# GpSimd sums of squares, and a halved last unit ahead of a norm, in a two-layer float32 encoder

## The chip, the cores and the metric

The kernel runs on 1 core of one Trainium2 chip. The time is the device time of one execution in microseconds (us), here the median of several runs. Engines are named as in the profile: PE is TensorE's matmul, PEld its weight load, DVE is VectorE, ACT is ScalarE, POOL is GpSimd, SP is SyncE, which issues the transfers.

## The reference

An encoder of two layers works on 256 tokens of width 2048. The part that matters here:

```python
for l in range(DEPTH):
    mod = (c_act @ w_mod[l] + b_mod[l]).reshape(bn, 6, d)
    ...
    h = layer_norm(x) * (1.0 + scale_m) + shift_m
    proj = h @ w_in[l]
    uv, q_c, kv_c, k_r, sb, sc, sh, ag = jnp.split(proj, IN_SPLITS, axis=-1)
    y_a = gmlp_mixer(uv, ...)
    y_b = mla_mixer(q_c, kv_c, k_r, ...)   # begins with rms_norm(q_c), rms_norm(kv_c)
    y_c = short_conv_mixer(sb, sc, sh, ...)
    y_d = conformer_conv(ag, ...)
    y = jnp.concatenate([y_a, y_b, y_c, y_d], axis=-1) @ w_out[l]
    x = layer_norm(ALPHA * x + (1.0 + gate_m) * y, post_mix_g[l], post_mix_b[l])

    h = layer_norm(x) * (1.0 + scale_f) + shift_f
    y = conv_ffn(h, ...)                   # ends in @ w_down
    x = layer_norm(ALPHA * x + (1.0 + gate_f) * y, post_ffn_g[l], post_ffn_b[l])
```

`rms_norm(x)` divides each token's row by the root of its mean square (384 columns for `q_c`, 256 for `kv_c`). Each layer has two products that end in a residual step and a LayerNorm over the 2048 columns of a token: `@ w_out` and `@ w_down`.

## The kernel before, in words

**Tokens and layout.** The 256 tokens are two tiles of 128 rows, `X[0]` and `X[1]`, kept on chip (in the instruction lists below they are called `x_97` and `x_98` at the place shown). The mixing groups A to D work with channels on the partitions and 256 tokens in the free direction.

**Products.** Most float32 products are made of three: ScalarE casts a block of weights to a rounded `hi` (L458), VectorE subtracts to get the rest, `lo` (L459), and TensorE adds hi*hi, hi*lo and lo*hi. Weight tiles are called `whi`/`wlo`, or `thi`/`tlo` where they lie in another pool. Some blocks are plain float32 instead (`wexact`), which the profile counts as two records for each product. All products go through one line, L83.

**Order.** The code is written as a stream: `stream` issues the load of one unit of weights and then runs the work that was pending, so loads run one unit ahead. Code order is not engine order: the framework's scheduler orders each engine's instructions by its own estimate of when they are ready, then every engine runs its list in order, waiting on semaphores.

**`out_proj`** makes both `@ w_out` (named o in the profile) and `@ w_down` (named d), so it runs four times; I name these o0, d0, o1, d1. The 2048 output columns go in three chunks, `CHUNKS = ((0, 1024), (1024, 512), (1536, 512))`. A bank of PSUM holds 512 columns of one token tile; `o_153600` is the bank of columns 1536 to 2047 of tile 0, `o_153610` that of tile 1. In the last chunk the last four units are kept in `state["tail"]`, and `done` runs them for tile 0 and then for tile 1, so that tile 0 ends early. A unit of this chunk has 4 blocks of 128 rows: 12 products of 512 columns for a tile (4 where the weights are plain float32).

After that, `finish` and `finish_bank` evacuate each tile's bank: `yg` = PSUM * gate (L704), `x` = ALPHA * x + `yg` (L707), and the statistics of the 512 columns (bn_stats, L710). Then the norm of the tile: `second(0)` for tile 0, `norm(1)` for tile 1. These aggregate the statistics, scale the rows and hand them to the next stage, which scales again (`xn`, L86) and transposes on TensorE (L597). At the end of the program (`then` is None) both tiles go through `norm`, which sends each 512 columns to the output; there tile 1 is the last work. An order dependency keeps tile 1's evacuation behind tile 0's norm, except at the end of the program.

**`mix_b`** starts with five squares of 128x256 (`sqB`, L1050, three for `q_c` and two for `kv_c`, two squares to a tile of 512 columns). Their sums over channels are one-column products against ones into `ps_ss`: for each token tile three accumulate for `q_c` and two for `kv_c`, ten in all. VectorE makes `rr` out of them (L1069, L1072), and GpSimd takes the power -0.5 (L114). TensorE fills waits here with products of group C (`C_c`).

Of the kernel before, what the change touches and what calls it, by code (L numbers as in the profile page):

```python
# [10 lines left out]
ALU = mybir.AluOpType  # L11
AX = mybir.AxisListType

P = 128
# [40 lines left out]
def encoder_kernel(ctx: ExitStack, tc: tile.TileContext, A: dict, consts: bass.AP, out: bass.AP):  # L55
# [20 lines left out]
    def ms_tile(name):  # L76
        return msp.tile([P, 512], F32, tag="ms", name=name)
# [39 lines left out]
    X = []  # L117
# [548 lines left out]
    def out_proj(l, w, src, order, gate_of, name, post_g, post_b, before, then, plain={}, bg=0):  # L666

        nkt = len(order)
        stats = [new_stats(f"{name}{t}") for t in range(2)]
        box, kept = {}, {}  # L670

        def products(t, item, ps, u, nk):
            parts, acts = item
# [19 lines left out]
        evacs = []  # L693

        def finish(t, ps, c0):
            for i in range(len(ps[t])):
                finish_bank(t, i, ps, c0)

# [91 lines left out]
        for c0, width in CHUNKS:  # L790
            last = c0 + width == D
            nk = 2048 // width
            units = nkt // nk
            state = {"tail": []}

            def load(u, c0=c0, width=width, nk=nk, units=units, last=last):
                kt = order[nk * u]
                assert order[nk * u : nk * u + nk] == list(range(kt, kt + nk))
                spare = nk if last and units - 4 <= u < units - 2 else 0
                exact = u < plain.get(c0, 0)  # L800
                parts = weights(w, kt, nk, c0, width, exact, spare)
                s4 = src[kt // 4]
                if exact:
                    return parts, [(s4[:, kt % 4 + k, :], None) for k in range(nk)]
                acts = []
                for k in range(0, nk, 2):
                    pair = kept.get(kt + k)
                    if pair is None:
                        pair = act_pair("a")
                        split(pair, s4[:, kt % 4 + k : kt % 4 + k + 2, :])  # L810
                        if nkt == KT:
                            kept[kt + k] = pair
                    for j in range(2):
                        acts.append([h[:, j, :] for h in pair[:2]])
                return parts, acts

            def unit(item, u, state=state, c0=c0, width=width, nk=nk, last=last, units=units):
                if u == 0:
                    state["ps"] = [
                        [acc_tile(f"{name}_{c0}{t}{i}") for i in range(width // 512)] for t in range(2)  # L820
                    ]
                if last and u >= units - 4:
                    state["tail"].append((item, u))
                    if evacs:
                        evacs.pop(0)()
                    return
                for t in range(2):
                    products(t, item, state["ps"], u, nk)
                if evacs:
                    evacs.pop(0)()  # L830

            for u in range(units):
                stream(lambda: load(u), lambda item, u=u, unit=unit: unit(item, u), bg, not last)

            def done(state=state, c0=c0, nk=nk, last=last):
                if c0 == 0:
                    box["gate"] = gate_of()
                if c0 + 512 == D - 512:
                    gains()
                for t in range(2):  # L840
                    for item, u in state["tail"]:
                        products(t, item, state["ps"], u, nk)
                while evacs:
                    evacs.pop(0)()
                if not last:
                    evacs.extend(
                        lambda t=t, i=i: finish_bank(t, i, state["ps"], c0)
                        for t in range(2)
                        for i in range(len(state["ps"][t]))
                    )  # L850
                    evacs.pop(0)()
                    return
                if before is not None:
                    before()
                for t in range(2):
                    finish(t, state["ps"], c0)
                    (norm if t == 1 or then is None else second)(t)
                if then is not None:
                    then(box)

            pending.append(done)


    def mixers(l, w_in, Y, hF=None, between=None):
# [163 lines left out]
        def mix_b(cps, _):  # L1028
# [30 lines left out]
            kc, ks = tmp_tile("kc"), None  # L1059
            dve.tensor_tensor(out=kc[0:64, 0:S], in0=ps[0:64, o : o + S], in1=cosT[0:64, :], op=ALU.mult)  # L1060
            dve.tensor_tensor(out=kc[0:64, S : 2 * S], in0=ps[0:64, o : o + S], in1=sinT[0:64, :], op=ALU.mult)
            ps = ms_tile("ps_ss")
            for t in range(2):
                for j in range(3):
                    mm(ps[:, t : t + 1], sqs[j][:, t * P : (t + 1) * P], ones[:, 0:1], j == 0, j == 2)
                for j in range(2):
                    mm(ps[:, 2 + t : 3 + t], sqs[3 + j][:, t * P : (t + 1) * P], ones[:, 0:1], j == 0, j == 1)
            rr = smallp.tile([P, 8], F32, tag="rr", name="rr")
            dve.tensor_scalar(  # L1069
                out=rr[:, 0:2], in0=ps[:, 0:2], scalar1=1.0 / Q_LORA, scalar2=RMS_EPS, op0=ALU.mult, op1=ALU.add  # L1070
# [551 lines left out]
```

## Time and profile before

| | |
|---|---|
| time, median of 3 runs | 2278.2 us (2276.4 to 2282.6) |
| profiled execution: its own time | 2274.61 us |
| its span in the trace | 2272.8 us |
| mean granted clock of TensorE | 0.994 |
| data moved | 605.19 MB, mean 266 GB/s |

All durations of the trace are from the one profiled execution, which lies 3.6 us under the median of the runs. Start times count from the start of the span. Layer 0 runs to about 1187 us (d0's norm), layer 1 behind it.

### The profile page before, as it was taken

What the parts mean: (1) busy time and instruction counts of PE and PEld (TensorE: products, weight loads), DVE (VectorE), ACT (ScalarE), POOL (GpSimd) and SP (SyncE); (2) the same over time, 40 slices, a digit from 0 to 9 for tenths busy, and PEclk for the clock granted to TensorE, in tenths of its full rate; (3) what the DMA queues carried; (4) which work ended last, traced back from release to release, by engine and by line L of the source; (5) the groups of instructions that cost most, each with busy time, mean ns of one, the idle gap of its engine ahead of it and who ended that gap; (6) DMA issues with size and microseconds to landing.
All of it is one profiled execution on the core that took longest, in us unless ns stands there. A gap on an engine that the chain in (4) does not pass through costs nothing.

```text
span 2272.8 us, 31376 instructions
## 1 busy us (share of the span) xinstructions
PE 2229.4 (98%) x12311; PEld 1919.6 (84%) x12311; DVE 1780.5 (78%) x2195; ACT 1107.0 (49%) x1652; POOL 35.1 (2%) x65
## 2 busy tenths in 40 slices
PE   7999999999999999999999999999999999999998
PEld 5788886788888888888789999889888888888886
DVE  5778988878888888989977899887775565565776
ACT  3356642354455444544554434545544454454553
POOL 0011000000000000000000000000000000000000
PEclk9999999999999999999999999999999999999999
DMA  9999699778888888899867677775675555555554
GB/s 350 388 371 361 254 327 360 245 275 315 310 313 313 309 317 325 300 343 328 296 235 251 203 242 248 281 269 178 232 258 185 190 187 198 185 187 197 187 188 148
DMA packets 228717, 605.19 MB, mean 266 GB/s; under 512 B 14661, under 2 KB 27189, under 8 KB 210901
## 3 DMA queue, kind: packets, MB, share of 16 engines
q1 hardware_dynamic: 227784, 602.30, 74.2%
q8 instruction: 96, 1.57, 0.3%
q0 software_dynamic: 784, 0.90, 0.1%
q14 instruction: 53, 0.43, 0.0%
HBM read 601.05 MB, written 2.10 MB: 265 GB/s over the span
## 4 chain that ended last, share of the span: by engine, by line
PE 89%; DVE 6%; DMA 2%; issue 1%; ACT 1%; POOL 0%; SPq 0%; DVEq 0%; ACTq 0%; POOLq 0%
PE g_c L83 22%; PE v_c L83 22%; PE d L83 19%; PE o L83 7%; PE C_c L83 4%; PE D_c L83 4%; PE B_c L83 2%; DVE wlo L459 1%; PE U_c L83 1%; PE E L83 1%; PE E_c L83 1%; PE U L83 1%; PE V L83 1%; DMA wmod<-in_w_mod_dram 1%; DVE macc L251 1%
## 5 line engine op out<-in xcount | busy, mean ns | idle before, releaser
L458 ACT CAST whi<-wraw 128x1024 fp32r<-128x1024 f32 (+1 forms) x632 | 643.3, 1043 | 751.6 <-PE g_c L83 221.7
L459 DVE TENSOR_TENSOR wlo<-wraw,whi 128x1024 fp32r<-128x1024 f32 (+1 forms) x632 | 750.3, 1213 | 302.7 <-ACT whi L458 283.1
L83 PE MATMUL d<-whi,a 128*128 128x512 f32 x1344 | 388.5, 390 | 2.3 <-ACT whi L458 2.3
L251 DVE SCALAR_TENSOR_TENSOR macc<-wmod,cact,macc 128x2048 f32<-128x2048 f32 (+2 forms) x174 | 353.7, 2033 | 24.4 <-DMA wmod<-in_w_mod_dram 23.7
L83 PE MATMUL v_c<-hT,whi 128*128 128x512 f32 (+1 forms) x1456 | 343.1, 383 | 0.0
L83 PE MATMUL g_c<-hT,whi 128*128 128x512 f32 (+1 forms) x1344 | 313.3, 380 | 0.0
L83 PEld LDWEIGHTS v_c<-hT,whi 128*128 128x128 f32 x1456 | 264.5, 189 | 48.5
L83 PEld LDWEIGHTS d<-whi,a 128*128 128x128 f32 x1344 | 251.7, 188 | 55.7 <-ACT whi L458 3.5
L83 PEld LDWEIGHTS g_c<-hT,whi 128*128 128x128 f32 x1344 | 243.4, 189 | 43.2
L83 PE MATMUL d<-wlo,a 128*128 128x512 f32 x672 | 233.5, 390 | 1.7 <-DVE wlo L459 1.7
L83 PE MATMUL v_c<-hT,wlo 128*128 128x256 f32 x1400 | 190.7, 283 | 0.0
L83 PEld LDWEIGHTS v_c<-hT,wlo 128*128 128x128 f32 x1400 | 183.1, 191 | 6.6
L83 PE MATMUL g_c<-hT,wlo 128*128 128x256 f32 x1280 | 175.8, 283 | 0.0
L83 PEld LDWEIGHTS g_c<-hT,wlo 128*128 128x128 f32 x1280 | 168.2, 191 | 5.9
L83 PEld LDWEIGHTS d<-wlo,a 128*128 128x128 f32 x672 | 126.1, 188 | 30.5 <-DVE wlo L459 4.3
L478 ACT CAST a<-g 128x512 fp32r<-128x512 f32 x132 | 80.7, 619 | 81.9 <-PE d L83 80.2
L83 PE MATMUL o<-whi,a 128*128 128x512 f32 x384 | 110.5, 392 | 0.5 <-ACT whi L458 0.5
L479 DVE TENSOR_TENSOR a<-g,a 128x512 fp32r<-128x512 f32 x132 | 87.5, 683 | 5.4 <-ACT a L478 5.4
L251 DVE SCALAR_TENSOR_TENSOR qacc<-wmod,cact,qacc 128x1024 f32<-128x1024 f32 (+1 forms) x75 | 80.3, 1071 | 11.6 <-DMA wmod<-in_w_mod_dram 9.2
L83 PEld LDWEIGHTS o<-whi,a 128*128 128x128 f32 x384 | 72.0, 188 | 16.9 <-ACT whi L458 1.3
L83 PE MATMUL D_c<-hT,whi 128*128 128x256 f32 x432 | 83.0, 292 | 2.2 <-ACT hT L478 1.6
L1381 DVE SCALAR_TENSOR_TENSOR u<-g,pf,u 128x254 f32<-128x254 f32 (+1 forms) x176 | 73.5, 478 | 0.0
(370 smaller groups left out, 2618.1 us busy)
## 6 DMA issues: line engine op xcount, KB each, us to landing
wraw<-in_ffn_w_up_dram SPq DMA_DIRECT2D x168, 1024.0 KB, 4.9
wmod<-in_w_mod_dram SPq DMA_DIRECT2D x134, 1024.0 KB, 6.0
wraw<-in_ffn_w_down_dram SPq DMA_DIRECT2D x88, 1024.0 KB, 5.3
wraw<-in_w_in_dram SPq DMA_DIRECT2D x33, 1024.0 KB, 7.5
wmod<-in_w_mod_dram SPq DMA_DIRECT2D x64, 512.0 KB, 9.2
wraw<-in_w_out_dram SPq DMA_DIRECT2D x26, 1024.0 KB, 5.2
wmod<-in_w_mod_dram SPq DMA_DIRECT2D x32, 768.0 KB, 8.0
wexact<-in_w_in_dram SPq DMA_DIRECT2D x46, 512.0 KB, 7.4
```

The costliest lines, as they stand in the source:

```text
L83: pe.matmul(o, lhsT, rhs, start=start, stop=stop, skip_group_check=True)
L251: i = dve.scalar_tensor_tensor(out=acc, in0=w, scalar=col, in1=acc, op0=ALU.mult, op1=ALU.add)
L458: act.copy(hi[:, :m], r)
L459: i = dve.tensor_tensor(out=lo[:, :m], in0=r, in1=hi[:, :m].bitcast(F32), op=ALU.subtract)
L478: act.copy(hi, src)
L479: dve.tensor_tensor(out=lo, in0=src, in1=hi.bitcast(F32), op=ALU.subtract)
L1381: dve.scalar_tensor_tensor(out=u[:, sh:], in0=x[:, : S - sh], scalar=col(k, j), in1=u[:, sh:], op0=ALU.mult, op1=ALU.add)
```

## The change

There are two edits. In `mix_b` three additions on GpSimd first add the squares (0 += 1, 3 += 4, 0 += 2), and one-column products are made of the sums alone: four instead of ten.

In `out_proj` the tile that the norm waits for (`first_ready`: tile 0, or tile 1 at the end of the program) has the products of the very last unit issued in two column halves of 256 (`halved`), and its bank is evacuated in two halves: multiply and residual step for columns 0 to 255, then for 256 to 511, then one bn_stats over all 512.

```diff
+        first_ready = 1 if then is None else 0
+
+        def halved(t, item, ps, h):
+            parts, acts = item
+            cols = slice(h * 256, (h + 1) * 256)
+            for k, (hi, lo) in enumerate(parts):
+                ahi, alo = acts[k]
+                end = k == len(parts) - 1
+                pairs = [(ahi, hi)] if lo is None else [(ahi, hi), (ahi, lo), (alo, hi)]
+                for i, (x, y) in enumerate(pairs):
+                    mm(ps[t][0][:, cols], x[:, t * P : (t + 1) * P], y[:, cols], False, end and i == len(pairs) - 1)
...
         def finish(t, ps, c0):
+            if t == first_ready:
+                for h in range(2):
+                    y = tmp_tile("yg")[:, :256]
+                    lo = c0 + h * 256
+                    xs = X[t][:, lo : lo + 256]
+                    dve.tensor_tensor(
+                        out=y, in0=ps[t][0][:, h * 256 : (h + 1) * 256], in1=box["gate"][:, lo : lo + 256], op=ALU.mult
+                    )
+                    dve.scalar_tensor_tensor(out=xs, in0=xs, scalar=ALPHA, in1=y, op0=ALU.mult, op1=ALU.add)
+                dve.bn_stats(out=stats[t][:, c0 // 512, :], in_=X[t][:, c0 : c0 + 512])
+                return
             for i in range(len(ps[t])):
                 finish_bank(t, i, ps, c0)
...
                 for t in range(2):
                     for item, u in state["tail"]:
-                        products(t, item, state["ps"], u, nk)
+                        if last and t == first_ready and u == units - 1:
+                            for h in range(2):
+                                halved(t, item, state["ps"], h)
+                        else:
+                            products(t, item, state["ps"], u, nk)
...
+            for into, other in ((0, 1), (3, 4), (0, 2)):
+                pool.tensor_tensor(out=sqs[into], in0=sqs[into], in1=sqs[other], op=ALU.add)
             ps = ms_tile("ps_ss")
             for t in range(2):
-                for j in range(3):
-                    mm(ps[:, t : t + 1], sqs[j][:, t * P : (t + 1) * P], ones[:, 0:1], j == 0, j == 2)
                 for j in range(2):
-                    mm(ps[:, 2 + t : 3 + t], sqs[3 + j][:, t * P : (t + 1) * P], ones[:, 0:1], j == 0, j == 1)
+                    mm(ps[:, 2 * j + t : 2 * j + t + 1], sqs[3 * j][:, t * P : (t + 1) * P], ones[:, 0:1], True, True)
```

In the lists of instructions below a row is line, operation, output<-inputs, size of the output and, where asked for, the semaphores that the instruction waits on.

VectorE at d0's evacuation of tile 0, before. `d_153600` is tile 0's bank, `gate_5` the gate, `x_97` tile 0's rows, `st_d` the statistics:

```order
L704 TENSOR_TENSOR yg<-d_153600_9139,gate_5_5016 128x512 [waits PE_49]
L707 SCALAR_TENSOR_TENSOR x_97<-x_97,yg 128x512 [waits DVE_49]
L710 BN_STATS st_d_7674<-x_97 128x6 [waits DVE_49]
L574 BN_AGGR mv_d0p_9565<-st_d_7674 128x2 [waits DVE_49]
L576 TENSOR_SCALAR rs_d0p_9567<-mv_d0p_9565 128x1 [waits DVE_49]
```

The same place after:

```order
L712 TENSOR_TENSOR yg<-d_153600_9143,gate_5_5020 128x256 [waits PE_49]
L712 TENSOR_TENSOR yg<-d_153600_9143,gate_5_5020 128x256
L715 SCALAR_TENSOR_TENSOR x_97<-x_97,yg 128x256 [waits DVE_49] x2
L716 BN_STATS st_d_7678<-x_97 128x6 [waits DVE_49]
L574 BN_AGGR mv_d0p_9584<-st_d_7678 128x2 [waits DVE_49]
```

Both half multiplies now stand ahead of both half residual steps; only the first has a wait on TensorE, and that wait is for the last product of the bank, both halves included.

TensorE at the tail of o1, before, from where tile 1's products (`o_153610`) begin to stand between those of tile 0 (`o_153600`); `thi`, `tlo` are weights that came earlier, `whi`, `wlo` those of the last units:

```order
L83 MATMUL o_153600_12604<-whi,a 128x512
L83 MATMUL o_153610_12605<-tlo,a 128x512
L83 MATMUL o_153610_12605<-thi,a 128x512 x2
L83 MATMUL o_153610_12605<-tlo,a 128x512
L83 MATMUL o_153600_12604<-wlo,a 128x512
L83 MATMUL o_153600_12604<-whi,a 128x512 x2
L83 MATMUL o_153600_12604<-wlo,a 128x512
L83 MATMUL o_153600_12604<-whi,a 128x512 x2
L83 MATMUL o_153600_12604<-wlo,a 128x512
L83 MATMUL o_153600_12604<-whi,a 128x512 x2
```

The same place after:

```order
L83 MATMUL o_153600_12620<-whi,a 128x256
L83 MATMUL o_153610_12621<-tlo,a 128x512
L83 MATMUL o_153610_12621<-thi,a 128x512 x2
L83 MATMUL o_153610_12621<-tlo,a 128x512
L83 MATMUL o_153610_12621<-thi,a 128x512
L83 MATMUL o_153600_12620<-wlo,a 128x256
L83 MATMUL o_153600_12620<-whi,a 128x256 x2
L83 MATMUL o_153600_12620<-wlo,a 128x256
L83 MATMUL o_153600_12620<-whi,a 128x256 x2
L83 MATMUL o_153610_12621<-thi,a 128x512
L83 MATMUL o_153610_12621<-tlo,a 128x512
L83 MATMUL o_153600_12620<-wlo,a 128x256
```

Before, four products of tile 1 stand between tile 0's first product of the last unit and its other eleven; after, five stand there and two more six halves later, with 17 halves of tile 0 behind them.

TensorE at the tail of o0, whose last units are plain float32, before (`yb`, `yc`, `yd` are the mixed activations of groups B, C, D):

```order
L83 MATMUL o_153600_2773<-wexact,yb 128x512 x4
L83 MATMUL o_153600_2773<-wexact,yc 128x512 x4
L83 MATMUL o_153600_2773<-wexact,yd 128x512 x4
L83 MATMUL o_153610_2774<-wexact,yb 128x512 x4
L83 MATMUL o_153610_2774<-wexact,yc 128x512 x4
```

The same place after:

```order
L83 MATMUL o_153600_2770<-wexact,yb 128x512 x4
L83 MATMUL o_153600_2770<-wexact,yc 128x512 x4
L83 MATMUL o_153600_2770<-wexact,yd 128x256 x2
L83 MATMUL o_153610_2771<-wexact,yb 128x512
L83 MATMUL o_153600_2770<-wexact,yd 128x256 x6
```

One product of tile 1 has moved in between the half products of tile 0. At d0 and d1 the order of the products is as before, but for the halving.

TensorE at the sums of squares of layer 1, before (`sqB` are the squares, three tiles):

```order
L83 MATMUL ps_ss<-onesR,sqB_11018 128x1 x2
L83 MATMUL ps_ss<-onesR,sqB_11019 128x1 x2
L83 MATMUL C_c_11231<-hT,whi 128x256 x2
L83 MATMUL C_c_11231<-hT,wlo 128x256
L83 MATMUL C_c_11231<-hT,whi 128x256
L83 MATMUL ps_ss<-onesR,sqB_11020 128x1
L83 MATMUL ps_ss<-onesR,sqB_11018 128x1 x2
L83 MATMUL ps_ss<-onesR,sqB_11019 128x1 x2
L83 MATMUL ps_ss<-onesR,sqB_11020 128x1
```

The same place after:

```order
L83 MATMUL ps_ss<-onesR,sqB_11037 128x1
L83 MATMUL C_c_11247<-hT,whi 128x256 x2
L83 MATMUL C_c_11247<-hT,wlo 128x256
L83 MATMUL C_c_11247<-hT,whi 128x256 x2
L83 MATMUL C_c_11247<-hT,wlo 128x256
L83 MATMUL C_c_11248<-hT,whi 128x256 x2
L83 MATMUL ps_ss<-onesR,sqB_11038 128x1
L83 MATMUL ps_ss<-onesR,sqB_11037 128x1
L83 MATMUL ps_ss<-onesR,sqB_11038 128x1
```

Four one-column products stand there, and between the first and the other three eight products of `C_c` instead of four. GpSimd's queue at the same place, after (before, it holds the two memsets and the power `rr` alone):

```order
L1089 TENSOR_TENSOR sqB_11037<-sqB_11037 128x256 [waits DMAHW1_49,PE_49,Activation_49]
L1089 TENSOR_TENSOR sqB_11037<-sqB_11037,sqB_11038 128x256 [waits Activation_49,Pool_49]
L1117 MEMSET rope 64x256 [waits PE_49,Pool_49]
L1089 TENSOR_TENSOR sqB_11038<-sqB_11038,sqB_11039 128x256 [waits Activation_49,Pool_49]
L1118 MEMSET rope 64x256
L114 TENSOR_TENSOR rr<-rr,mhalf 128x4 [waits DVE_49]
```

A memset of `rope` now stands between the second and the third add. In layer 0 the three adds stand together ahead of both memsets, and one of the four one-column products ahead of two `C_c`, three behind them. The orders on ScalarE and of the transfers are unchanged; on VectorE, besides the norms, some steps of layer 1's mixing change places.

More of the change, by code (lines that the diff above doesn't have):

```diff
@@ L833, in out_proj, with done @@
                 stream(lambda: load(u), lambda item, u=u, unit=unit: unit(item, u), bg, not last)
-            def done(state=state, c0=c0, nk=nk, last=last):
+            def done(state=state, c0=c0, nk=nk, last=last, units=units):
                 if c0 == 0:
```

## The prediction

> **What bounds the kernel now.** I read the busy shares of the page first (busy us, share of the span, instructions), then the shares of the chain of work that ended last.
>
> ```profile
> PE 2229.4 (98%) x12311; PEld 1919.6 (84%) x12311; DVE 1780.5 (78%) x2195; ACT 1107.0 (49%) x1652; POOL 35.1 (2%) x65
> PE 89%; DVE 6%; DMA 2%; issue 1%; ACT 1%; POOL 0%; SPq 0%; DVEq 0%; ACTq 0%; POOLq 0%
> ```
>
> TensorE sets the end for 89% of the span, so a change is worth what it takes from the products or from the stretches in which TensorE waits. The four norms behind `out_proj` are such stretches. I call them o0, d0, o1, d1 (mixing and feed-forward of layers 0 and 1). Two views of d0: the chain (start, length, engine, tile, line, count), then the timeline, in which a bracket gives the idle time ahead and what ended it:
>
> ```profile
> 1171.87 2.96 PE d L83 x13
> 1174.86 0.70 DVE yg L704
> 1175.58 0.70 DVE x L707
> 1176.31 0.70 DVE st_d L710
> 1185.42 1.53 ACT xn L86 x2
> ```
> ```profile
> 1186.29 1.36 PE L597 MATMUL ps_xT<-cst,xn 128*128 128x128 f32 x8 [0.59 <-ACT xn L86]
> ```
>
> Tile 0's last product ends at 1174.83. The evacuation (L704), residual (L707) and statistics (L710) follow one after the other, and 10 us later TensorE stands 0.59 us for the scaled rows `xn`. So what delays tile 0 here delays everything. At the end of the program (d1) tile 1 stands in that place, with nothing beside it.
>
> **The halved evacuation on VectorE.** Before, from L704's start to the statistics' start is 1176.31 - 1174.86 = 1.45 us. The change has two multiplies of 256 columns, two residual steps of 256, then the statistics. Timeline rows of that width, from layer 1's mixing:
>
> ```profile
> 1343.53 0.42 DVE L1109 TENSOR_TENSOR qc<-ps_qr,cst 128x256 f32<-128x256 f32 x1
> 1343.87 0.42 DVE L1110 TENSOR_TENSOR qc<-ps_qr,cst 128x256 f32<-128x256 f32 x1
> 1333.99 5.76 DVE L891 SCALAR_TENSOR_TENSOR convD<-gluD,pm,convD 128x230 f32<-128x230 f32 x15
> ```
>
> A multiply from PSUM starts 0.34 us after the one ahead; a three-operand step takes 5.76 / 15 = 0.38, the last one about 0.46 to its end. Sum: 2 x 0.34 + 0.38 + 0.46 + 0.02 (semaphore) = 1.54 us, so +0.09. It would be a gain only if the first half left while the second half's products run. The order (VectorE piece above) speaks against it: the second multiply has no wait on TensorE of its own, so the first one's wait already covers the last product. Both start after it.
>
> **The halved products on TensorE.** 12 products of 512 columns become 24 of 256. Two rows of the chain:
>
> ```profile
> 2019.92 119.71 PE d L83 x528
> 1400.81 17.28 PE E_c L83 x144
> ```
>
> At 512 columns one takes 119.71 / 528 = 0.227 us, at 256 columns 17.28 / 144 = 0.120. 24 x 0.120 - 12 x 0.227 = +0.16 us. For d0 and d1, where nothing else moves: +0.16 + 0.09 = **+0.25 us each**. Ends: 0 (halves cost exactly half on both engines) and +0.55 (no overlap between the four short steps, 4 x 0.46 against 1.45).
>
> **o1.** Here the order on TensorE moves too (piece above): three more of tile 1's products stand ahead of tile 0's end. The timeline there:
>
> ```profile
> 1503.39 2.00 ACT L458 CAST whi<-wraw 128x1024 fp32r<-128x1024 f32 x2 [4.57 <-DMA wraw<-in_w_out_dram]
> 1504.47 2.36 DVE L459 TENSOR_TENSOR wlo<-wraw,whi 128x1024 fp32r<-128x1024 f32 x2 [2.11 <-ACT whi L458]
> 1505.75 0.19 PEld L83 LDWEIGHTS o<-wlo,a 128*128 128x128 f32 x1 [0.26 <-DVE wlo L459]
> 1508.60 0.69 DVE L704 TENSOR_TENSOR yg<-o,gate 128x512 f32<-128x512 f32 x1 [1.77 <-PE o L83]
> 1519.63 1.36 PE L597 MATMUL ps_xT<-cst,xn 128*128 128x128 f32 x8 [2.01 <-ACT xn L86]
> ```
>
> The last weights land late: the two `whi` are cast at about 1504.4 and 1505.4, the two `wlo` ready at about 1505.70 and 1506.85. New sequence: first product from 1504.45 to 1504.57, five of tile 1 (1.13 us) to 1505.71, six halves (0.72) to 1506.45, two of tile 1 to 1506.90, 17 halves (2.04) to 1508.95. Tile 0 ended at 1508.57 before: +0.38 us, and +0.09 on VectorE. TensorE waits 2.01 us at the end of this chain, so nothing hides it: **+0.47**. Ends +0.10 (the extra tile 1 products fit into waits) and +0.80 (all three, 0.68, and the 0.16 of the halves, in full).
>
> **o0.** Its last products are plain float32, two records each, in the timeline:
>
> ```profile
> 401.80 3.60 PE L83 MATMUL o<-wexact,yd 128*128 128x512 f32 x8
> 405.43 0.69 DVE L704 TENSOR_TENSOR yg<-o,gate 128x512 f32<-128x512 f32 x1 [5.25 <-PE o L83]
> 415.73 0.69 DVE L704 TENSOR_TENSOR yg<-o,gate 128x512 f32<-128x512 f32 x1 [0.23 <-PE o L83]
> 428.31 0.66 PE L597 MATMUL ps_xT<-cst,xn 128*128 128x128 f32 x4 [0.79 <-ACT xn L86]
> ```
>
> The eight records run without a gap, 0.43 us each, so the weights are there; halving costs nothing in float32. But one 512-column product of tile 1 now stands between the second and third half product: 2 x 0.43 = 0.86 us later for tile 0. Tile 1's evacuation is next in VectorE's queue and has 0.23 us of slack. So 0.86 + 0.09 - 0.23 = **+0.72**; TensorE waits for tile 1's norm at 428.31. Ends 0 (a later wait takes it up) and +0.95 (no slack).
>
> **The sums of squares, layer 1.** Ten one-column products become four; three adds of 128x256 go to GpSimd, in front of them. First ACT's timeline, then TensorE's part of the chain:
>
> ```profile
> 1323.58 0.66 ACT L1050 ACTIVATE sqB<-B_c 128x256 f32<-128x256 f32 x2 [1.00 <-PE B_c L83]
> 1324.48 0.67 ACT L1050 ACTIVATE sqB<-B_c 128x256 f32<-128x256 f32 x2
> 1325.74 0.42 ACT L1050 ACTIVATE sqB<-B_c 128x256 f32<-128x256 f32 x1
> ```
> ```profile
> 1325.70 0.79 PE ps_ss L83 x8
> 1326.49 0.58 PE C_c L83 x4
> 1327.07 1.23 PE ps_ss L83 x12
> ```
>
> Each product is two records: 20 records took 2.02 us, 12 of them go, 1.2 us. No row shows an add of this size on GpSimd. The nearest are two groups of GpSimd's instructions (busy us, mean ns) and three timeline rows of o0's norm:
>
> ```profile
> L1091 POOL MEMSET rope<- 64x256 f32 x2 | 0.6, 306 | 4.8 <-PE ps_mix L83 4.7
> L114 POOL TENSOR_TENSOR rr<-rr,mhalf 128x4 f32<-128x4 f32 x2 | 2.1, 1054 | 60.6 <-DVE rr L1072 60.6
> ```
> ```profile
> 407.98 1.41 DVE L737 SCALAR_TENSOR_TENSOR x<-x,mv_o0p,gb 128x512 f32<-128x512 f32 x2
> 408.14 0.99 POOL L114 TENSOR_TENSOR rs_o0p<-rs_o0p,mhalf 128x1 f32<-128x1 f32 x1 [105.48 <-DVE rs_o0p L576]
> 414.74 0.56 POOL L114 TENSOR_TENSOR rs_o0r<-m_o,mhalf 128x1 f32<-128x1 f32 x1 [5.61 <-DVE m_o L760]
> ```
>
> Lower end 0.31 (256 columns written, none read); upper end 1.05 plus two more passes of 0.31, 1.7 us. The last rows show one power of one column at 0.99 us beside VectorE's work and at 0.56 without. VectorE is busy at both places of the adds, so I take the two-operand row under load, **0.9 us**. [...]
>
> With 0.9: first add 1324.27 to 1325.17, second to 1326.09. TensorE reaches the first product at 1325.70 and stands till 1326.13, then runs that (0.24) and eight `C_c` (0.96) to 1327.33. The third add waits for the last square (1326.16) and the moved memset, ends 1327.33; three products, done 1328.07. Before, 1328.30 with four `C_c` fewer: -0.23 - 4 x 0.12 = **-0.7**. Ends: -1.2 (add at 0.31 to 0.5, no wait) and +1.7 (add at 1.7). The `C_c` that moved behind `ps_qn` and the reordered conv taps on VectorE are the same instructions and fill the same waits: 0.
>
> **The sums of squares, layer 0.** The timeline at the products, a stretch behind them (each engine's busy us and count: PE, PEld, DVE, ACT, POOL; granted clock; DMA share; GB/s), and a step of the chain:
>
> ```profile
> 217.02 0.63 ACT L1050 ACTIVATE sqB<-B_c 128x256 f32<-128x256 f32 x2
> 220.38 0.37 ACT L1050 ACTIVATE sqB<-B_c 128x256 f32<-128x256 f32 x1
> 220.80 1.85 PE L83 MATMUL ps_ss<-onesR,sqB 128*128 128x1 f32 x12 [0.30 <-ACT sqB L1050]
> ```
> ```profile
> 221.72:228.54 6.82, 6.82 (x20) 5.65 (x20) 6.52 (x12) 6.38 (x17) 0.12 (x1) 0.50 1.01 416
> ```
> ```profile
> 274.41 6.92 DMA wmod<-in_w_mod_dram
> ```
>
> The adds would end at 218.60, 219.52 and, after the late last square, 221.70; the products at about 222.6, against 222.65 before. The saved products turn into a wait: **0**, ends -0.75 and +1.0. The chain goes over the transfer of `wmod` at 274, which takes up part of either. If that cover is gone, the ends count in full.
>
> **Sum.** 0 + 0.72 + 0.25 - 0.7 + 0.47 + 0.25 = +1.0 us; the ends add to -1.85 and +5.55. The profiled execution took 2274.6 us (span 2272.8) and lies 3.6 under the median of the runs, 2278.2; on the median I predict **2279.2**.
>
> **Rivals.** (1) The halves do overlap: the first half's multiply and residual step go under the second half's products. Then the statistics start about 0.9 us after the last product, not 1.45; 4 x (-0.55 - 0.09) = -2.6, time 2276.6. Against it: the single wait. 0.06. (2) The low clock vanishes. The windows row shows a granted clock of 0.50 for the 6.8 us behind layer 0's one-column products. At full clock that work is done in half, -3.4, unless the transfer at 274 takes it back: 2275.8. For it: six of ten such products go. Against: TensorE stands in their place. [...] 0.12. (3) The adds cannot run well beside VectorE and TensorE stands for them in both layers. With 3 us an add, the working above gives +4.9 in layer 0 and +5.6 in layer 1, with the norms' +1.7 in all +12: 2290. It is slower by over 0.3% from about 2.1 us an add. For it: 0.99 against 0.56. Against: the 0.99 us power ended while VectorE's pair still ran. 0.08.
>
> **Chances.** The forecast has 0.74. A change of 0.3%, 6.8 us, is about what a measurement of this kernel can tell from none. Forecast and rivals 1 and 2 stay inside, save a little where both add up (faster 0.04); rival 3 is slower (0.08). The range reaches below rival 2 and to the upper end of the sum plus a little run-to-run spread: 2274 to 2285.
>
> **What would show it.** In the profile after: both 256-column multiplies of a norm start after tile 0's last product, statistics 1.5 to 1.6 us behind the first; tile 0's evacuation at o0 some 0.9 us later in its stage; GpSimd adds near 0.9 us with TensorE waiting for them; four one-column products a layer. A first multiply that starts a microsecond or more before the last product, adds over 2 us, or a stage between 220 and 230 at full clock would make me wrong.

## The result, and the profile after

The changed kernel takes 2282.64 us (median of 20 runs, 2277.9 to 2288.19), the kernel before 2277.6 (20 runs, 2271.77 to 2282.95). The ratio is 1.0023, 95% interval 1.0017 to 1.0030: about 5 us slower, where +1.0 was forecast. The time lies inside the range and the change is under 0.3%, as forecast, but the loss is five times the sum. So the question is where the other 4 us come from.

The page after, its busy shares and its chain:

```profile
PE 2230.3 (98%) x12331; PEld 1923.6 (84%) x12331; DVE 1784.1 (78%) x2203; ACT 1106.9 (48%) x1652; POOL 43.4 (2%) x71
PE 83%; DVE 9%; DMA 4%; issue 2%; ACT 2%; POOL 0%; SPq 0%; DVEq 0%; ACTq 0%; POOLq 0%
```

TensorE's busy time is nearly the same (2229.4 before), but its share of the chain fell from 89 to 83%. The time went into waits. The profiled execution has a span of 2282.6 us, 9.8 more than the profiled one of before. I laid the two traces over each other, product by product, and read where the distance grows: 3.1 us at layer 0's sums of squares and 0.5 to 1 us more up to 305, 0.9 at o0, 1.7 near 1130, 0.3 at d0, 1.1 between the sums of layer 1 and 1430, 2.4 at o1, 0.3 at the end. The rest is a few tenths of both signs. Three of these places need explaining: layer 0's sums, o1, and the one near 1130, which the change does not touch at all.

**The halves at o0.** The tile's last product, then the two multiplies and the statistics:

```profile
407.01 2.75 PE L83 MATMUL o<-wexact,yd 128*128 128x256 f32 x12
```
```profile
409.80 0.76 DVE L712 TENSOR_TENSOR yg<-o,gate 128x256 f32<-128x256 f32 x2 [6.13 <-PE o L83]
411.26 0.69 DVE L716 BATCH_NORM_STATS2 st_o<-x 128x6 f32<-128x512 f32 x1
```

The last product ends at 409.76, and both multiplies come behind it.

**Layer 0's sums.** GpSimd's adds in the timeline after, then VectorE's steps and TensorE's products there:

```profile
217.29 1.62 POOL L1089 TENSOR_TENSOR sqB<-sqB 128x256 f32<-128x256 f32 x1 [21.30 <-ACT sqB L1076]
218.99 4.28 POOL L1089 TENSOR_TENSOR sqB<-sqB,sqB 128x256 f32<-128x256 f32 x2
```
```profile
217.14 1.20 DVE L939 TENSOR_TENSOR convD<-convD,prodD 128x992 f32<-128x992 f32 x1
218.24 2.83 DVE L251 SCALAR_TENSOR_TENSOR macc<-wmod,cact,macc 128x2048 f32<-128x2048 f32 x1
220.99 1.70 DVE L939 TENSOR_TENSOR convD<-convD,prodD 128x988 f32<-128x988 f32 x1
```
```profile
221.70 0.59 PE L83 MATMUL ps_ss<-onesR,sqB 128*128 128x1 f32 x2 [3.38 <-POOL sqB L1089]
```

The three adds take 1.62, 2.65 and 1.67 us, not 0.9. Each begins inside a step of VectorE and ends some 0.6 us after it; the step of VectorE that follows is longer than its like (2.83 against 2.35, 1.70 against 1.18). TensorE stands 3.38 us. The windows of 3.41 us behind it (busy us of PE, PEld, DVE, ACT, POOL; granted clock; DMA share; GB/s):

```profile
217.64:221.05 3.41, 0.67 (x4) 0.24 (x2) 3.41 (x3) 3.04 (x9) 3.33 (x2) 1.00 1.03 338
221.05:224.47 3.42, 2.77 (x9) 2.42 (x10) 3.42 (x5) 1.74 (x5) 2.83 (x4) 0.50 1.03 423
224.47:227.88 3.41, 3.41 (x11) 2.87 (x12) 3.36 (x6) 3.41 (x9) 0.00 (x0) 0.50 0.99 410
227.88:231.29 3.41, 3.41 (x10) 2.69 (x9) 3.17 (x8) 3.41 (x10) 1.02 (x1) 0.50 1.04 429
```

A window in which TensorE works 0.67 us is followed by three at half clock. Two windows there were at half clock before, too (the row with 0.50 in the prediction), and the window ahead of those had only 0.30 us without work:

```profile
218.37:221.78 3.41, 3.11 (x23) 2.63 (x21) 3.41 (x3) 2.75 (x8) 0.00 (x0) 1.00 1.06 391
```

So the low clock here does not need the stand, and the change has one window of it more. The last section says what such windows have in common.

**Near 1130** TensorE waits in both kernels for the same weights, 1.65 and 0.60 us a microsecond apart. Windows of before, then of after:

```profile
1126.32:1129.73 3.41, 2.17 (x10) 1.47 (x8) 3.41 (x8) 1.83 (x3) 0.00 (x0) 1.00 0.61 234
1129.73:1133.15 3.42, 2.41 (x9) 1.72 (x10) 3.42 (x6) 3.21 (x4) 0.00 (x0) 1.00 0.04 14
1133.15:1136.56 3.41, 3.41 (x16) 2.82 (x15) 3.41 (x6) 0.62 (x1) 0.00 (x0) 1.00 0.80 268
```
```profile
1132.41:1135.82 3.41, 1.15 (x5) 0.44 (x4) 3.41 (x8) 3.10 (x4) 0.00 (x0) 1.00 0.04 16
1135.82:1139.24 3.42, 3.42 (x9) 2.65 (x10) 3.42 (x5) 1.31 (x2) 0.00 (x0) 0.50 0.35 81
```

All edges of the granted clock in a trace lie on one grid of 3.413 us (in all 14 traces to 3 ns), whose phase differs from execution to execution (here the edges stand at 1129.73 before and at 1132.41 after, which is no whole number of steps apart); the expectations of e5 and e12 call one step of it an activity window. Before, the edge at 1129.73 cut through the first wait: each window has over 2 us of work, and the clock stays full. After, both lie in one window with 1.15 us of work, and the next runs at half clock: 9 products instead of 16, 1.7 us lost. Nothing was done to this place; it was dealt another phase.

**o1** has both. Its wait for `xn` grew from 2.01 to 2.66 us by the change. Before, the grid cut it in two; after, it fell into one window. Windows of before, then of after:

```profile
1515.44:1518.85 3.41, 2.19 (x10) 1.49 (x8) 2.53 (x12) 1.61 (x5) 0.56 (x1) 1.00 0.98 330
1518.85:1522.27 3.42, 2.59 (x20) 2.27 (x21) 3.28 (x7) 3.38 (x8) 0.97 (x1) 1.00 1.01 367
```
```profile
1524.95:1528.36 3.41, 0.70 (x6) 0.46 (x5) 2.55 (x8) 2.06 (x5) 0.55 (x1) 1.00 1.03 363
1528.36:1531.77 3.41, 3.41 (x16) 3.41 (x17) 3.34 (x8) 3.41 (x9) 0.98 (x1) 0.50 1.05 402
```

From 40 to 2250 us the trace of before has 6 windows at half clock, that of after 10; at 1.7 us each (half of 3.413) where TensorE sets the pace, up to 6.8 of the 9.8 us between these two executions are clock.

### The profile page after: what moved, and what is told of

Read it like the earlier page. It is cut to its first block, busy times and chain, and to the rows that moved or that the text cites. A ratio compares the mean times of both kernels' runs of the same rounds, so it can differ in the third digit from the quotient of the medians.

```text
span 2282.6 us, 31438 instructions
## 1 busy us (share of the span) xinstructions
PE 2230.3 (98%) x12331; PEld 1923.6 (84%) x12331; DVE 1784.1 (78%) x2203; ACT 1106.9 (48%) x1652; POOL 43.4 (2%) x71
## 4 chain that ended last, share of the span: by engine, by line
PE 83%; DVE 9%; DMA 4%; issue 2%; ACT 2%; POOL 0%; SPq 0%; DVEq 0%; ACTq 0%; POOLq 0%
PE g_c L83 22%; PE v_c L83 22%; PE d L83 18%; PE C_c L83 4%; PE D_c L83 3%; PE o L83 3%; DVE wlo L459 2%; DMA wmod<-in_w_mod_dram 2%; PE U_c L83 1%; DVE macc L251 1%; DMA wraw<-in_w_out_dram 1%; PE E L83 1%; DVE convD L917 1%; PE B_c L83 1%; PE V L83 1%
## 5 line engine op out<-in xcount | busy, mean ns | idle before, releaser
L83 PE MATMUL d<-whi,a 128*128 128x512 f32 (+1 forms) x1360 | 390.4, 388 | 2.3 <-ACT whi L458 2.3
L83 PE MATMUL d<-wlo,a 128*128 128x512 f32 (+1 forms) x680 | 235.8, 389 | 1.9 <-DVE wlo L459 1.9
L83 PE MATMUL o<-whi,a 128*128 128x512 f32 (+1 forms) x392 | 111.0, 388 | 0.9 <-ACT whi L458 0.8
```

The lines of the kernel that those rows point to most:

```text
L83: pe.matmul(o, lhsT, rhs, start=start, stop=stop, skip_group_check=True)
```

## The experiments

Theory A: the loss is stands of TensorE, above all for adds of GpSimd that VectorE holds up, and half clock in the window behind a stand. Rivals: the halves cost it (B), chance alone (C). All ratios are to the kernel before, on the same chip, with 95% intervals.

**The parts, each alone.**

```diff
 e1: only the edit in mix_b          e3: the same, in layer 1 only:   + if l == 1:
 e2: only the edit in out_proj       e12: the same, in layer 0 only:  + if l == 0:
```

> The sums of squares alone changed (GpSimd adds, four one-column products), norms as before. Theory A (TensorE stands for adds that cannot run well beside VectorE in layer 0, and the convolution steps of VectorE that the adds hold up in layer 1 come late): most of the loss is here, +3 to +5 us over the kernel before; in the trace TensorE stands 3 to 4 us ahead of the first one-column product of layer 0, adds of 1.5 us or more there and under 1 us in layer 1. Rival B (the loss is the norms' halves): within 1 us of before. Rival C (the loss is chance: low-clock stretches that fall differently in every execution): within 1 us of before in the median, with the same spread of times and the same mean granted clock.

Measured: 2281.5 against 2279.44 us, ratio 1.0008 (0.9999 to 1.0017): +2 us, under the +3 to +5 of A, and the interval does not exclude C. The mean granted clock over the executions is the same as before (0.9916 and 0.9917). The adds in layer 0 took 1.62, 2.65 and 1.67 us again, and TensorE stood 3.39 us. In layer 1 the first add was not under 1 us here. GpSimd's and VectorE's timeline:

```profile
1324.79 2.78 POOL L1063 TENSOR_TENSOR sqB<-sqB 128x256 f32<-128x256 f32 x1 [30.29 <-ACT sqB L1050]
1327.64 0.76 POOL L1063 TENSOR_TENSOR sqB<-sqB,sqB 128x256 f32<-128x256 f32 x1
```
```profile
1324.62 2.36 DVE L459 TENSOR_TENSOR wlo<-wraw,whi 128x1024 fp32r<-128x1024 f32 x2
1326.89 3.39 DVE L891 SCALAR_TENSOR_TENSOR convD<-gluD,pm,convD 128x235 f32<-128x235 f32 x5
```

It began 0.17 us behind the start of a pair of subtractions and ended some 0.6 us after the pair. In the first profile of the changed kernel it came 0.04 us after the end of the pair and took 0.94. So layer 1's price depends on where that pair stands when the squares are done, and the traces have two such places, some 2.2 us apart.

> The halved products and evacuation alone, sums of squares as before. Theory A: the terms as predicted, o0 +0.7 to +0.9, d0 +0.35, o1 +0.5, d1 +0.2, so +1.5 to +2 us over before, and up to 1 us more where a longer wait at a norm brings a stretch of low clock. Rival B: +4 to +5 us. Rival C: within 1 us. First multiply of each halved evacuation after the last product in all theories.

Measured: ratio 1.0000 (0.9991 to 1.0008). The terms stand in the trace (first multiply behind the last product at all four norms), but the sum does not show in the time. B falls: +4 to +5 us would be 1.002. A and C are not told apart: +1.5 us would be 1.0007, inside the interval.

> The sums of squares changed in layer 1 alone. Theory A: +0.5 to +1.5 us over before, so the rest of the first kernel's loss (2 to 4 us) is layer 0's; adds under 1 us, VectorE's five convolution steps beside them about 3.4 us long instead of 2.0. If layer 1 behaves as predicted: -0.7. Rival C: within 1 us of before for both kernels.

Measured: ratio 1.0000 (0.9990 to 1.0010), adds of 0.94, 0.78 and 0.80 us in the profiled execution. +0.5 to +1.5 and -0.7 both lie in the interval, so this run does not tell them apart.

> The sums of squares changed in layer 0 alone, all else as before. Theory A (an add of GpSimd waits for the rest of VectorE's running step and then runs 0.6 us): adds of 1.62, 2.65 and 1.67 us again, TensorE standing 3.4 us ahead of the first one-column product, two to three activity windows of low clock behind it; with layer 1's sums alone at no change, this part carries what the sums cost: +2 to +4 us over before. Rival (the loss needs all parts together): within 1 us of before.

Measured: 2281.3 against 2279.34, ratio 1.0010 (1.0001 to 1.0019), 2 us; the lower edge of what A expects, and the interval reaches into the rival's 1 us. Adds and stand as in the changed kernel:

```profile
218.56 1.62 POOL L1064 TENSOR_TENSOR sqB<-sqB 128x256 f32<-128x256 f32 x1 [21.31 <-ACT sqB L1050]
220.27 4.28 POOL L1064 TENSOR_TENSOR sqB<-sqB,sqB 128x256 f32<-128x256 f32 x2
```

Layer 0's sums are the only part that is slower by itself beyond its interval. Half clock behind them: 2 or 3 windows in each of the five traces that have these adds (12 in all), against 5 windows in the seven traces with the sums as before on the same engines. From ahead of these sums (about 210 us) to about 290 us, TensorE falls behind the trace of before by 2.4 to 4.1 us in each of the five (2.7 in e12); in the six other traces with the old sums it moves by between -1.1 and +0.3 us.

**The whole once more.**

> The changed kernel itself once more, beside the kernel before and on one chip with the next kernel, so that the parts can be added up on equal terms. Theory A (the loss is made of stands of TensorE, and of low-clock stretches that follow a stand of some 2 us or more inside one activity window): 1.001 to 1.003 of before, TensorE standing 3.4 us ahead of layer 0's sums again, adds of about 1.6, 2.7 and 1.7 us there again because VectorE's steps stand at the same places; the low-clock stretches lie elsewhere than in the first profile, but behind the same few waits. Rival C (chance): within 0.1% of before, other waits low.

Measured: 2283.58 against 2280.02, ratio 1.0018 (1.0009 to 1.0027). Layer 0 as expected; in layer 1 the first add took 2.76 us this time. Near 1130 the waits were cut apart by the grid (0.95 and 1.29 us) and the clock stayed full; at o1 2.53 us fell into one window and the next was at half clock. The parts add to 1.0008 +- 0.0012, the whole is 1.002: that they act on each other, through the phases and longer waits, is possible and not shown. C falls with the 20 executions above (1.0017 to 1.0030).

**The same adds on VectorE.**

```diff
+                dve.tensor_tensor(out=sqs[into], in0=sqs[into], in1=sqs[other], op=ALU.add)
```

> The three adds issued on VectorE instead of GpSimd, four one-column products, norms as before. The scheduler sets two products of group C ahead of layer 0's one-column products here. Theory A (two engines that hold each other up are the cost, not the adds): adds of about 0.42 us, TensorE without the stand of over 3 us in layer 0, time -1 to +1.5 us against before. Rival D (any add that comes ahead of the products in series costs that much): +3 to +5 us, as with GpSimd.

Measured: 2286.46 (5 executions), ratio 1.0033 (1.0020 to 1.0045): worse than GpSimd, not what A expects, and by its median (+7 us) more than D does. The adds take 0.42 us, but the last two stand in VectorE's queue behind five convolution steps and end at 230.4; the products then wait for them (4.72 us), and `ps_rkv` for those (2.94 us). Three windows in a row in TensorE's share:

```profile
224.95:228.37 3.42, 0.90 (x5) 0.44 (x3) 3.42 (x6) 3.42 (x10) 0.00 (x0) 1.00 0.99 406
228.37:231.78 3.41, 1.22 (x6) 1.25 (x7) 3.07 (x5) 3.41 (x10) 0.00 (x0) 0.50 1.05 431
231.78:235.19 3.41, 0.62 (x3) 0.54 (x3) 1.84 (x7) 2.82 (x8) 1.79 (x1) 0.50 0.65 269
```

The clock stayed at half for 17 us. Neither theory has it right: what costs on VectorE is the place in its queue, not the 0.42 us of an add. So this run does not show what adds would cost on an engine that took them at once.

**What an add on GpSimd waits for.**

```diff
 e7:
-                pool.tensor_tensor(out=sqs[into], in0=sqs[into], in1=sqs[other], op=ALU.add)
+                pool.tensor_scalar(out=sqs[into], in0=sqs[into], scalar1=1.0, scalar2=None, op0=ALU.mult)
 e9, behind each tile's products in d1's first chunk:
+                        i = pool.tensor_tensor(out=tmp_tile("probe")[:, :S], in0=cst[:, 512:768], in1=cst[:, 768:1024], op=ALU.add)
+                        tc.add_manual_dep(i.ins, newest[0].ins.name, data_dep, reason="one after the other")
```

> As the sums alone, but each add on GpSimd replaced by an operation of the same size with one operand (times 1), which leaves the other squares out of the sums. Theory A1 (an operation of GpSimd with two operands in SBUF can only run while VectorE is not in a step with two such operands): these take about 0.5 to 0.8 us each in both layers, wherever they land, and TensorE stands under 2 us in layer 0. Rival A2 (any reading operation of GpSimd is held up by VectorE's long steps): 1.6 to 2.7 us in layer 0 as with the adds.

Measured in one execution: 2.01, 2.31 and 1.33 us in layer 0, 1.95, 0.85 and 0.93 in layer 1, TensorE standing 3.18 us. One operand does not help: this fits A2, not A1.

```profile
216.12 5.70 POOL L1063 TENSOR_SCALAR sqB<-sqB 128x256 f32<-128x256 f32 x3 [21.05 <-ACT sqB L1050]
```

> The kernel before with an add of 128x256 on GpSimd behind each tile's products of the first chunk of d1 (44 in all, results unused), a stretch in which VectorE alternates pairs of subtractions of 1024 columns (two operands in SBUF, 1.2 us each) with idle time. Theory A (GpSimd's reading operation waits for VectorE's running step and then holds up the next): adds that start while VectorE is idle take about 0.6 us; those that start inside a subtraction take the rest of that subtraction and some 0.6 us more, up to 1.9 us; the subtraction behind such an add is longer by about as much as the add itself runs. Rival (GpSimd is slow by itself, and the durations in layers 0 and 1 have another cause): all about the same, whatever VectorE does.

Measured in one execution. GpSimd's and VectorE's timeline, two adds each of a pattern that repeats through all 44:

```profile
2066.09 1.44 POOL L832 TENSOR_TENSOR probe<-cst 128x256 f32<-128x256 f32 x1 [1.72 <-PE d L85]
2068.81 1.00 POOL L832 TENSOR_TENSOR probe<-cst 128x256 f32<-128x256 f32 x1 [1.28 <-PE d L85]
```
```profile
2065.70 2.90 DVE L461 TENSOR_TENSOR wlo<-wraw,whi 128x1024 fp32r<-128x1024 f32 x2 [1.93 <-ACT whi L460]
2068.53 0.68 DVE L481 TENSOR_TENSOR a<-g,a 128x512 fp32r<-128x512 f32 x1
```

The first subtraction of the pair runs from 2065.70 to 2066.93. The add that starts at 2066.09 has 0.84 us of it ahead and takes 1.44; the one at 2068.81 has 0.40 us of a step ahead and takes 1.00. So an add takes the rest of VectorE's running step and 0.60 us, in all 44 within 0.01, and the pair is 2.90 us long instead of 2.59. That is less than expected: the next subtraction grows by 0.32 us, about half of the add's own 0.60. None of the 44 met an idle VectorE, so the 0.6 alone was not seen free-standing, and what Theory A says of it is untested. Layer 0's three adds follow the same rule: 1.05, 2.08 and 1.08 us of rest, plus 0.57 to 0.59. Where two subtractions stand without a gap (e1), the add waited for both; why not for both in the two convolution and modulation steps of layer 0 is left open.

It is so with one operand (e7, 1.33 to 2.31 us in layer 0) as with two (1.62 to 2.65). By which mechanism the two engines hold each other up is not shown.

**Filling TensorE's waits.** If half clock follows idle windows, work without use should keep it away.

```diff
+    def keep_busy(o, widths):
+        ahead = newest[0].ins.name
+        for n in widths:
+            mm(o[:, :n], ident, cst[:, 512 : 512 + n], True, True)
+            tc.add_manual_dep(newest[0].ins, ahead, order_dep, reason="only when nothing else is left")
 first_group, layer 1's feed-forward:  + keep_busy(cps[0], (512, 512))
 rest, ahead of the late transposes:   + keep_busy(ms_tile("warm"), (512, 128))
 out_proj, d0's last chunk:            + keep_busy(state["ps"][0][0], (512, 256))
```

> The kernel before with idle products put into three waits of TensorE that the trace shows (1.07 us of them into the 1.20 us behind the modulation's one-column products near 478, 1.29 into the 1.65 us at the start of d0's last chunk near 1128, 1.72 into the 2.01 us at o1's norm). Their results are overwritten or unused. Theory A: these waits then never bring low clock: full clock at 478 to 490, 1130 and 1523 in every execution, 3 to 6 us less than before, mean granted clock up by 0.002 or more. If the low clock has nothing to do with TensorE's idle time: same time as before, or up to 1 us more where an idle product is still running when the real one could start.

Measured: 2274.64 against 2280.02, ratio 0.9983 (0.9973 to 0.9993), mean granted clock over the executions 0.9955 against 0.9924. At 478 and o1 the idle products stand in the wait. At d0 they do not: they run at 1120.95, 7 us ahead of it, so that TensorE comes later to the wait, which is 0.30 us instead of 1.65. Windows at 477, 1128 and 1517 and behind two of them:

```profile
477.40:480.80 3.40, 3.06 (x18) 1.91 (x17) 0.94 (x2) 2.72 (x6) 0.00 (x0) 1.00 1.05 396
480.80:484.20 3.40, 3.06 (x14) 2.75 (x15) 3.07 (x7) 2.53 (x5) 0.00 (x0) 1.00 1.00 403
1128.00:1131.50 3.50, 2.71 (x11) 1.92 (x12) 3.50 (x6) 3.50 (x5) 0.00 (x0) 1.00 0.00 1
1517.60:1521.00 3.40, 2.68 (x12) 1.19 (x11) 2.91 (x7) 2.79 (x5) 0.58 (x2) 1.00 0.98 348
1521.00:1524.40 3.40, 3.40 (x31) 3.40 (x32) 3.40 (x6) 2.92 (x8) 0.72 (x1) 1.00 1.06 404
```

Between 40 and 2250 us only two windows near 80 are left at half clock. This is the fastest kernel of the study, 0.17% under the kernel before. The gain stands in the medians and not in this pair of traces: both have a span of 2272.8 us, since the profiled execution of before had full clock near 1130 and at o1 by its phase, and the idle products made the filled one 1.3 us later at o1.

> The changed kernel with the idle products of the filled kernel in the same three waits. Theory A: the change's stands remain (layer 0's sums with their low clock, layer 1's sums), the low clock behind the three waits goes: 3 to 6 us less than the changed kernel, so 0.999 to 1.001 of before, and still 4 us or more above the filled kernel without the change. If the change's loss were low clock at the norms alone: as fast as the filled kernel.

Measured: 2280.88 against 2277.39, ratio 1.0013 (1.0001 to 1.0024), above the expected 0.999 to 1.001: the idle products take about 0.0005 to 0.0010 off the change's 1.0018 and 1.0023, less than expected and not clear of the intervals. In its trace the three waits have full clock and layer 0's sums three windows at half. Against the filled kernel without the change the difference is 0.0030, some 7 us, with both intervals at +- 0.001: the change's loss does not go with these three waits.

**Halves that do overlap.**

```diff
-                    mm(ps[t][0][:, cols], ..., False, end and i == len(pairs) - 1)
+                    to = ps[t][0][:, cols] if h == 0 else box["own"][:, :256]
+                    mm(to, ..., h == 1 and k + i == 0, end and i == len(pairs) - 1)
 finish: multiply and residual step over the bank's 512 columns, then over box["own"]'s 256 (a plain add), then bn_stats
```

> Halved products, but the second half of the last unit accumulates in a PSUM bank of its own, whose 256 columns are multiplied and added at the end; the first 512 columns are evacuated before. Sums of squares as before. If the wait for a whole bank was what kept the halves from overlapping: at d0 and d1 the first multiply starts at least 1 us before the tile's last product, and from the last product to the statistics it is about 0.8 us instead of 1.5. If the scheduler or the reading engine waits anyway: both multiplies behind the last product, 1.9 us or more.

Measured in one execution, d0. The chain:

```profile
1177.65 0.70 DVE yg L711
1178.38 0.69 DVE x L712
1179.09 0.44 DVE yg L715
1179.55 0.44 DVE x L718
1180.01 0.70 DVE st_d L719
```

The first multiply starts 1.4 us ahead of the tile's last product, which ends at about 1179.05, and the statistics start 0.96 us behind it instead of 1.5 (expected: about 0.8). At d1 it is the same, 1.4 and 0.95 us. So a bank of its own lets the halves overlap. It is also a tile of its own in the program, so whether the bank or the tile decides where the program waits is not told apart.

> The filled kernel with the last unit's second half in a bank of its own (the evacuation that overlaps). Theory A: what d0, o1 and d1 gain by the earlier statistics (0.5 us each at most) is about what the halved products cost, so within 1 us of the filled kernel: 0.9975 to 0.9990 of before. If the overlap is worth what it saves at each of four norms: 2 us below the filled kernel, 0.9965 to 0.998.

Measured: 2274.96 against 2277.39, ratio 0.9986 (0.9975 to 0.9997), the same as the filled kernel within the interval: the overlap buys nothing measurable. And one miss for the filling: near 478 this execution had half clock again.

```profile
474.30:477.71 3.41, 3.41 (x27) 2.93 (x26) 2.52 (x3) 0.96 (x3) 0.00 (x0) 1.00 1.05 393
477.71:481.12 3.41, 2.79 (x12) 2.26 (x11) 1.00 (x4) 2.91 (x7) 0.00 (x0) 0.50 1.05 419
```

By the rows TensorE was busy all through the window ahead, but 2.2 us of it are the modulation's one-column products. They seem to count for nothing; the last section has the count over all traces.

## Why the prediction was right or wrong, point by point

- **Both halves wait for the last product: right.** At all four norms the first multiply starts behind it, and from it to the statistics it is 1.45 or 1.46 us, against 1.54 forecast: halving the evacuation costs nothing and gains nothing. Rival 1 did not happen.
- **o0, +0.72: right in mechanism, +0.9 in the first trace.** Tile 0 ends 0.87 us later in its stage, the one product of tile 1 (0.86). The 0.23 us of slack that I took off was not there.
- **d0 and d1, +0.25 each: +0.3 each.** Right.
- **o1, +0.47: the step was too small and it missed its consequence.** Tile 0's evacuation starts 0.85 us later, 0.05 over the upper end. The weights came 0.17 later at this place, and the sum left out that the last half product ends 0.16 us behind the 0.12 us step at which the halves follow each other (17 of them in 2.04 us, as forecast). What the sum had no term for is the clock: a wait of 2.0 us becomes 2.66, and where enough of it lies in one window the next runs at half clock and costs 1.7 us more. The longer wait had it in three of three traces, the wait of 2.0 us in four of seven; that the change makes it more likely is not shown by so few.
- **Layer 0's sums, 0 (-0.75 to +1.0): the step that failed.** I took 0.9 us for an add by the row of a one-column power under load. Measured 1.62, 2.65 and 1.67 us, 5.9 in sum against 2.7. The row showed that VectorE matters and not how: the price is the rest of VectorE's step, and in layer 0 the steps are 1.2 and 2.35 us long. The adds end at 218.91, 221.64 and 223.27 instead of 218.60, 219.52 and 221.70, in a trace that is 0.4 us ahead at this place. The transfer of `wmod` that I counted on to hide part of a loss hid none: behind it, at 290, the first trace is 4.1 us further back than ahead of the sums. Rival 3 had the mechanism and the sign; its price of 3 us an add was too high, and the mean here, 1.98, is just under the 2.1 that it needed.
- **Layer 1's sums, -0.7: +1.1 in the first trace.** There the adds took 0.94, 0.78 and 0.80 us, as forecast, and TensorE stood 0.47 us for the first. But the adds hold up VectorE too: five convolution steps took 3.42 us instead of 1.97, and TensorE waits 0.56 us at `ps_rkv`, where it did not wait before. I named VectorE as a load on the add and not the add as a load on VectorE. Together that is +0.4 us, in e3's trace as well. The other 0.7 is a wait of 0.64 us at 1428 (`ps_var`, behind the convolution). Only the two traces of the changed kernel have it (0.92 in e5); e3, with the same adds in layer 1, has none, so these adds alone do not bring it, and its cause stays open. Where the first add took 2.8 us, TensorE fell 4.9 (e1) and 2.9 us (e5) behind from 1300 to 1380, half clock included. So the size of this term is a matter of chance, and 0.4 is its cheap case.
- **Rival 2, the low clock vanishes: the place was right, the cause in part.** Behind layer 0's unchanged sums it was there in some executions and not in others (0 windows in e2, e3, e6 and e9, two in e8), so it goes with the grid's phase: how much of the one-column products and of the waits falls into one window (1.55 to 1.66 us in e2, e3, e6 and e9, 1.79 to 2.21 in before, e8 and e11). In the changed kernel TensorE's stand takes the place of the six products. And where it was missing, TensorE stood 1.85 us at `ps_rkv` instead, so only about 1.3 us of the 3.4 came back.
- **The time:** the sum of +1.0 left out some 4 us; that the median still lies inside the range owes to the range, not to the terms. Shown as a cause: layer 0's adds (the stand in all five traces, 2 us alone in e12, though its interval goes from 0.2 to 4.3 us). Not settled: how much of the rest is layer 1's adds, which take 0.94 or 2.8 us by chance, and how much is half clock. An estimate for the clock: in e5's round the mean granted clock is 0.9907 with the change and 0.9924 without, and among the executions of the kernel before one is 0.75 to 1.2 us longer for each 0.001 of clock less (by round), which gives 1.3 to 2.1 of the 4 us.

## What to carry to other kernels

An idle engine is not a free one: before work goes to GpSimd, look at what VectorE runs at that place, and price each add there at the rest of VectorE's running step plus its own time (0.57 to 0.60 us here, for 256 columns), and VectorE's next step at 0.3 to 0.5 us more (e9 and layer 0). A wait of TensorE, taken together with one-column products beside it, can cost a second time where about half a window of 3.413 us goes to them (here half clock followed all 48 windows with 1.93 us or more); price it with that chance, and try work without use in the wait before any change of the arithmetic. The halves of an evacuation overlapped here only when they lay in different banks and tiles (e8), and even then the gain did not beat the cost of the halved products measurably (0.9986 of before, against 0.9983 for the filled kernel without it).

## What the hardware showed that I had not expected

- The grid of 3.413 us has a phase of its own in each trace, so a single one need not stand for its kernel: the executions of the kernel before have mean granted clocks of 0.989 to 0.996 and are 0.75 to 1.2 us longer for each 0.001 less, 5 to 8 us from the highest clock to the lowest by my estimate. At the two plain waits, near 1130 and at o1, over 14 traces: 13 windows held 1.68 us of idle time or more, and the next was at half clock each time; all windows with 1.54 us or less were followed by full clock. So about half a window decides.
- Idle time alone does not tell which windows: some with no idle time were followed by half clock (e11 above), and four with 1.83 to 1.85 us by full clock (`ps_rkv` in e2, e3, e6 and e9). It comes out once products of one and four columns are counted as no work. Over the windows from 40 to 2250 us of the 14 traces, of those at full clock with 1.93 us or more without a wider product all 48 were followed by half clock, of those with 1.67 us or less none (8895); of the 16 in between, seven. A window at half clock was followed by another one in all 39 cases with 0.62 us or more of such time, and with 0.57 us or less in one case of 56. That fits the two or three windows at half clock behind layer 0's sums, where the one-column products lie in the next window too. It is a count over this kernel's traces, and no run was made to test it.
- Idle products at three places, 1.1 to 1.7 us of TensorE each, which add work, made the kernel 0.17% faster.
- Memsets on GpSimd took 0.30 and 0.31 us beside the same kind of steps of VectorE that held the adds up.
